# Two layers of a decoder trunk: layer 1's projections run four steps ahead through one queue, and a head's row of maxima comes by transposes alone

## The chip, the cores and the metric

The kernel runs on one core of one Trainium2 chip. The metric is the device time of one execution in microseconds (us); the time of a kernel is the median of its runs. A difference of 0.3% (9.2 us here) is about what a measurement of this kernel can tell from no change.

## What is computed

Two layers on x of 2048 rows by 1024 columns, float32. Layer 0 is a gated linear recurrence beside a pooling mixer. Layer 1, which the change touches, is attention with 16 heads of 64 columns, cut to:

```
proj = h @ w_in                                  # q, k, v, gate, forget logit
q, k = rms_norm per head;  cumf = cumsum(log_sigmoid(fl + b_f))
logits = q·k * scale + cumf[query] - cumf[key]   # causal
o = softmax(logits) @ v * silu(gate);  x = x + gate * (o @ w_out)
```

A softmax over a row may have any one number taken from all logits of the row: the quotient stays the same. The kernel takes the row's maximum, so that the exponentials stay in range.

## The kernel before

The 2048 rows go in four segments s = 0 to 3 of 512. For each segment layer 0 runs, then layer 1. The 512 new queries of a segment meet the keys of segments 0 to s; old keys and values come back from DRAM (`k1d`, `k2d`, `vd`). A product of float32 numbers is made of several fp32r products of a high and a low part, so a projection step is 24 matmuls (8 depth blocks by 3 passes) of 256 columns.

**One head of layer 1.** `prep` transposes the projected q and k of a head (`pqkT`) and builds four operands. `Q1` and `K1` hold 64 rows of the high part and 64 of the low part. `Q3` and `K2` hold the rest in 68 rows: 64 of high part, and four more. In these four, `K2` has the forget sum's high and low part and two rows of ones, `Q3` has two rows of ones and two rows for the negated maximum's high and low part. These last two rows are zero at first (a transfer from `q4d`). `max_pass` multiplies `Q3` by `K2` in blocks (`pmx`), takes the maximum of each on VectorE (`mxs`, `m`: 128 queries by 4 blocks), makes a negated high and low part (`mh`, `mhl`), turns them by one transpose into 8 rows of 128 (`pmt`), copies these to SBUF (`mr`) and sends them by a transfer from ScalarE's queue into rows 66 and 67 of `Q3`. `attend` then adds two products per block of 128 keys in PSUM (`pst`), of which the second reads `Q3` with these rows, takes exponentials twice on ScalarE (`ph` in fp32r, and `pst` in float32), their difference on VectorE (`pl`), a running sum on GpSimd (`la`), and multiplies by the values (`pov`, `pol`).

**The order.** The program is written as generators that are interleaved, and the framework orders each engine's instructions ahead of time from it. `quad_attention` runs four heads; while head h attends, the maxima of head h+1 are taken step by step, the last part of `max_pass` (from `pmt` on) comes behind `attend`, and `prep` of head h+2 behind that. `need` takes steps of the fill until a result is there. The fill of a quad of four heads is `quad_fill`: 16 steps of projections (q and k of a pair of heads, a gate, the next pair, the next quad's values), spread over the yields of the four heads by `weave`, and used up at the end of the quad. Each quad makes a new `Steps` queue. Since the 16 steps are spread over four heads, the q and k that `prep` needs behind an even head are projected during that very head. In the last quad of s = 0 to 2 the fill goes on with the first part of the next segment's layer 0 (`pre0`), in that of s = 3 with the output projection (`out_most`). The first head's maxima are taken ahead of quad 0, beside two steps of the values.

Of the kernel before, what the change touches and what calls it, by code (L numbers as in the profile page):

```python
# [8 lines left out]
F32 = mybir.dt.float32  # L9
# [9 lines left out]
P = 128  # L19
# [6 lines left out]
NH = 16  # L26
HD = 64
VW = 2 * HD + 2
EPS = 1e-6
NEG = -1e30  # L30

# [2 lines left out]
def trunk(ctx, tc, x, cvec, norm_g, ada_c, ada_w, ada_b, ada_bg, lbp, w0, w0o, w1, w1f, w1o,  # L34
# [115 lines left out]

    x1d = dr.tile([T, D], F32, name="x1d")
    k1d = dr.tile([NH, P, T], F32, name="k1d")
    k2d = dr.tile([NH, HD + 4, T], F32, name="k2d")
    vd = dr.tile([NH, P, T // P, VW], F32, name="vd")
    cfd = dr.tile([NH, 4, T], F32, name="cfd")
    q4d = dr.tile([4, SEG], F32, name="q4d")
    gd = dr.tile([2, D], F32, name="gd")


# [816 lines left out]
    def forget_rows(s, act):  # L976
        pf = ps_pj("pfl")

        for d in range(ND):
            for b in range(2):  # L980
                mm(pf[0:48, :], wf[:, d, :], act[:, d, b, :], start=(d + b == 0), stop=(d + b == ND))
        z = tmp("z")[0:NH]
        S.activation(z, pf[0:NH, :], AF.Identity, bias=fb)
        V.tensor_tensor(z, pf[32:32 + NH, :], z, op=ALU.add)
        a = tmp("za")[0:NH]
        S.activation(a, z, AF.Abs)
        S.activation(a, a, AF.Exp, scale=-1.0)
        S.activation(a, a, AF.Ln, bias=1.0)

        V.scalar_tensor_tensor(z, z, 0.0, a, op0=ALU.min, op1=ALU.subtract)  # L990
        cf = tmp("cf")[0:NH]
        V.tensor_tensor_scan(cf, z, zero1[0:NH].to_broadcast([NH, SEG]), fcar, op0=ALU.add, op1=ALU.add)
        V.tensor_copy(fcar, cf[:, SEG - 1:SEG])
        V.tensor_scalar(cf, cf, -1.0, None, op0=ALU.mult)
        ch_ = tmp("cfh", F32R)[0:NH]
        V.tensor_copy(ch_, cf)
        cl = tmp("cfl", F32R)[0:NH]
        split_lo(cl, cf, ch_)
        nc.sync.dma_start(cfd[:, 0, s * SEG:(s + 1) * SEG], f(ch_))
        nc.sync.dma_start(cfd[:, 1, s * SEG:(s + 1) * SEG], f(cl))  # L1000

    seg1 = [dict() for _ in range(NSEG)]

# [53 lines left out]
    def prep(s, h):  # L1057

        L = seg1[s]
        qk = L["qk", h // 2]  # L1060
        j = h % 2
        pt = ps_misc("pqkT")
        for tb in range(NTB):
            transpose(pt[:, tb * P:(tb + 1) * P], qk[:, tb, j * P:(j + 1) * P])
        lo, up = slice(0, HD), slice(HD, P)
        g = col["qkg"]
        Q1 = qp.tile([P, SEG], F32R, name="Q1", tag="qa")
        Q3 = qp.tile([P, SEG], F32R, name="Q3", tag="qb")
        K1 = kp.tile([P, SEG], F32R, name="K1", tag="k1c")
        K2 = kp.tile([P, SEG], F32R, name="K2", tag="k2c")  # L1070
        S.activation(Q1[lo], pt[lo], AF.Copy, scale=g[lo])
        S.activation(K1[up], pt[up], AF.Copy, scale=g[up])
        V.scalar_tensor_tensor(Q1[up], pt[lo], g[lo], f(Q1[lo]), op0=ALU.mult, op1=ALU.subtract)
        V.scalar_tensor_tensor(K1[lo], pt[up], g[up], f(K1[up]), op0=ALU.mult, op1=ALU.subtract)
        S.copy(Q3[lo], f(Q1[lo]))
        S.copy(K2[lo], f(K1[up]))
        nc.scalar.dma_start(f(Q3[HD:HD + 4]), q4d)
        nc.scalar.dma_start(f(K2[HD:HD + 4]), cfd[h, :, s * SEG:(s + 1) * SEG])
        if s < NSEG - 1:
            nc.sync.dma_start(k1d[h, :, s * SEG:(s + 1) * SEG], f(K1))  # L1080
            nc.sync.dma_start(k2d[h, :, s * SEG:(s + 1) * SEG], f(K2[0:HD + 4]))
        L["ops", h] = (Q1, Q3, K1, K2)

    def old_k2(h, c):
        K2 = kp.tile([P, SEG], F32R, name="K2o", tag="k2o", bufs=3)
        nc.sync.dma_start(f(K2[0:HD + 4]), k2d[h, :, c * SEG:(c + 1) * SEG])
        return K2

    def max_pass(s, h):

        _, Q3, _, K2 = seg1[s]["ops", h]
        mxs = small([P, NTB, NSEG], "mxs")
        for c in range(s + 1):
            kc = K2 if c == s else old_k2(h, c)
            for i in range(NTB):
                n = SEG if c < s else (i + 1) * P
                pm = ps_mx("pmx")
                mm(pm[:, 0:n], Q3[0:HD + 4, i * P:(i + 1) * P], kc[0:HD + 4, 0:n], start=True, stop=True)
                if c < s:
                    V.tensor_reduce(mxs[:, i, c:c + 1], pm[:, 0:n], axis=AX.X, op=ALU.max)  # L1100
                else:
                    V.tensor_tensor_reduce(pm[:, 0:n], pm[:, 0:n], mq[:, SEG - n:], 1.0, NEG, op0=ALU.add,
                                           op1=ALU.max, accum_out=mxs[:, i, c:c + 1])
                if c < s or i < NTB - 1:
                    yield
        m = small([P, NTB], "m")
        V.tensor_reduce(m, mxs[:, :, 0:s + 1], axis=AX.X, op=ALU.max)
        mhl = small([P, 2, NTB], "mhl")
        mh = small([P, NTB], "mh", F32R)
        V.tensor_scalar(mh, m, -1.0, None, op0=ALU.mult)  # L1110
        V.tensor_copy(mhl[:, 0, :], f(mh))
        V.scalar_tensor_tensor(mhl[:, 1, :], m, -1.0, f(mh), op0=ALU.mult, op1=ALU.subtract)
        yield
        pt = ps_misc("pmt")
        transpose(pt[0:2 * NTB, 0:P], mhl.rearrange("p a b -> p (a b)"))
        mr = sp.tile([2 * NTB, P], F32R, name="mr", tag="mr", bufs=1)
        V.tensor_copy(mr, pt[0:2 * NTB, 0:P])
        nc.scalar.dma_start(f(Q3[HD + 2:HD + 4].rearrange("a (b t) -> a b t", t=P)), f(mr))

    def attend(s, h):  # L1120

# [17 lines left out]
        for c in range(s + 1):  # L1139
# [8 lines left out]
            for b in range(NTB):  # L1148
                q0 = 0 if c < s else b * P
                ks = slice(b * P, (b + 1) * P)  # L1150
                st = ps_st("pst")
                mm(st[:, q0:], k1[:, ks], Q1[:, q0:], start=True, stop=False)
                mm(st[:, q0:], k2[0:HD + 4, ks], Q3[0:HD + 4, q0:], start=False, stop=(c < s))
                if c == s:
                    mm(st[:, q0:q0 + P], identb, mk, start=False, stop=True)
                ph = tmp("ph", F32R)
                S.activation(ph[:, q0:], st[:, q0:], AF.Exp)  # L1157
                S.activation(st[:, q0:], st[:, q0:], AF.Exp)  # L1158
                pl = tmp("pl", F32R)
                split_lo(pl[:, q0:], st[:, q0:], ph[:, q0:])  # L1160
                if kb == 0:
                    first = f(ph)
                    if s == 0:
                        G.tensor_copy(la, first)
                elif kb == 1 and s > 0:
                    G.tensor_tensor(la, first, f(ph), op=ALU.add)
                else:
                    G.tensor_tensor(la[:, q0:], la[:, q0:], f(ph[:, q0:]), op=ALU.add)  # L1168
                todo.append((b, q0, kb, vv, ph, pl))
                if len(todo) > LAG:  # L1170
                    values(*todo.pop(0))
                kb += 1
                yield
# [32 lines left out]
        L["pairs"] = pair + 1  # L1206

    LAG = 2

    def quad_attention(s, quad, fill):  # L1210

# [21 lines left out]
    def layer1(s, xs):  # L1233
# [12 lines left out]
        prep(s, 0)  # L1246
        next(vq)
        prep(s, 1)
        fill = Steps()
        fill.add(vq, 2)  # L1250
        fill.add(quad_fill(s, 0), 16)
        weave(max_pass(s, 0), NTB * (s + 1) + 1, fill, keep=16)
        L["mix"] = big.tile([P, ND, 2, SEG], F32R, name="o1", tag="act")
        for quad in range(4):
            if quad:
                fill = Steps()
            more = quad == 3 and s + 1 < NSEG
            if more:
                pre = pre0(s + 1)
                fill.add(take(pre, 2), 2)  # L1260
            n = 16 if quad < 3 else 8
            if s == 0 and quad == 1:
                fill.add(both(quad_fill(s, quad), ada_gate1()), n + 9)
            elif quad:
                fill.add(quad_fill(s, quad), n)
            if more:
                fill.add(pre, NPRE - 2)
            elif quad == 3:
                fill.add(out_most(s, L), 14)
            weave(quad_attention(s, quad, fill), 16 * (s + 1), fill, keep=2 if more else 0)  # L1270
        finish(s, NH - 1)
        fill.drain()
        if s == NSEG - 1:
# [8 lines left out]
    def constants():  # L1282
# [15 lines left out]
        V.memset(o1, 1.0)  # L1298
        z1 = tmp("z1")
        V.memset(z1, 0.0)  # L1300
        nc.sync.dma_start(q4d[0:2, :], o1[0:2])
        nc.sync.dma_start(q4d[2:4, :], z1[0:2])
        for s in range(NSEG):
            nc.sync.dma_start(cfd[:, 2, s * SEG:(s + 1) * SEG], o1[0:NH])
            nc.sync.dma_start(cfd[:, 3, s * SEG:(s + 1) * SEG], o1[0:NH])
        wfr = tmp("wfr", F32, (P, ND, NH))
        nc.sync.dma_start(wfr, w1f)
        V.tensor_copy(wf[:, :, 0:NH], wfr)
# [80 lines left out]
```

## Time and profile before

| | |
|---|---|
| median of 3 runs | 3062.76 us (3058.55 to 3068.89) |
| the profiled execution | 3059.16 us, span 3057.4 us |
| TensorE busy | 2799.8 us (92% of the span), mean granted clock 0.975 |
| VectorE, ScalarE, GpSimd busy | 2373.8, 1792.8, 1191.7 us |

The span is the time from the first to the last instruction. Each engine works off its instructions in order and waits at one whose input is not there yet; the profile names the instruction that ended the wait. Matmuls are pipelined: the busy time of one counts until its result is there, while the next has begun already.

### The profile page before, as it was taken

Reading aid. Unit: us, or ns where it says so; the run is one execution under the profiler, and the core shown is the slowest. Engines: PE = TensorE matmul, PEld = TensorE weight load, DVE = VectorE, ACT = ScalarE, POOL = GpSimd, SP = SyncE. Lnnn points to the kernel's source line nnn. Section 1 sums busy time; section 2 is a strip of 40 time slices with the busy share of each in tenths; the row PEclk is TensorE's granted clock in tenths of the full one; section 3 lists DMA queues with packets and bytes.
Section 4 is the critical chain, followed back from the end, with each engine's and each line's share of the span. In section 5 each row is a group of like instructions: output and inputs, shape, how many; then the busy total and the mean of one; then the engine's idle time right before and its main releaser. Section 6 shows DMA issues by size and latency. Waiting matters only on the chain.

```text
span 3057.4 us, 49147 instructions
## 1 busy us (share of the span) xinstructions
PE 2799.8 (92%) x17020; PEld 2378.7 (78%) x17020; DVE 2373.8 (78%) x4646; ACT 1792.8 (59%) x3679; POOL 1191.7 (39%) x992
## 2 busy tenths in 40 slices
PE   4999898999998898999999899989999999999998
PEld 4888877879887777779888677777888977676767
DVE  8877688867676888876677888888758688888886
ACT  3454566763545666674445666667544566666674
POOL 3321233323212444434111555554421246655565
PEclk9999999999999999999999999999999999999999
DMA  6423454424234334434234343443333323333342
GB/s 247 163 78 104 120 141 106 122 77 128 73 114 111 101 96 109 130 90 135 68 102 118 111 108 115 117 125 106 115 99 94 110 90 101 103 96 99 92 135 79
DMA packets 198904, 338.56 MB, mean 111 GB/s; under 512 B 19768, under 2 KB 67000, under 8 KB 196096
## 3 DMA queue, kind: packets, MB, share of 16 engines
q1 hardware_dynamic: 195264, 321.52, 36.3%
q10 hardware_dynamic: 3392, 13.90, 1.3%
q8 instruction: 135, 2.21, 0.3%
q14 instruction: 113, 0.93, 0.1%
HBM read 285.72 MB, written 49.36 MB: 110 GB/s over the span
## 4 chain that ended last, share of the span: by engine, by line
PE 49%; DVE 16%; DMA 6%; ACT 5%; issue 3%; POOL 0%; SPq 0%; DVEq 0%; ACTq 0%; POOLq 0%
PE py L40 9%; PE pst L40 6%; PE pgt L40 6%; PE pqk L40 6%; PE pv L40 4%; PE pmx L40 3%; DMA K2o<-k2d 3%; PE pov L40 3%; PE pol L40 2%; PE pq L40 2%; DVE pl L182 2%; PE pl L40 2%; PE pf L40 2%; DVE wt L182 2%; DMA Q<-mr 2%
## 5 line engine op out<-in xcount | busy, mean ns | idle before, releaser
L182 POOL TENSOR_TENSOR wt<-raw,wt 128x512 fp32r<-128x512 f32 x287 | 431.3, 1511 | 998.1 <-ACT wt L293 931.9
L1168 POOL TENSOR_TENSOR la<-la,ph 128x512 f32<-128x512 f32 (+3 forms) x528 | 614.6, 1164 | 445.4 <-ACT ph L1157 396.5
L1157 ACT ACTIVATE ph<-pst 128x512 fp32r<-128x512 f32 (+3 forms) x640 | 341.6, 534 | 277.6 <-PE pst L40 258.6
L182 DVE TENSOR_TENSOR pl<-pst,ph 128x512 fp32r<-128x512 f32 (+3 forms) x640 | 385.7, 604 | 123.2 <-ACT pst L1158 111.1
L40 PE MATMUL pqk<-wt,h 128*128 128x256 f32 x3072 | 457.4, 286 | 5.7 <-DVE h L495 2.6
L40 PEld LDWEIGHTS pqk<-wt,h 128*128 128x128 f32 x3072 | 426.4, 192 | 29.8 <-DVE h L495 3.4
L40 PE MATMUL pgt<-h,wt 128*128 128x512 f32 x1536 | 418.5, 406 | 0.2 <-ACT e L527 0.2
L293 ACT CAST wt<-raw 128x512 fp32r<-128x512 f32 x578 | 337.3, 622 | 72.2 <-PE py L40 33.3
L40 PE MATMUL pv<-wt,h 128*128 128x256 f32 x2304 | 346.9, 295 | 6.0 <-DVE h L182 4.3
L40 PEld LDWEIGHTS pv<-wt,h 128*128 128x128 f32 x2304 | 324.1, 200 | 22.7 <-DVE h L182 6.4
L1158 ACT ACTIVATE pst<-pst 128x512 f32<-128x512 f32 (+3 forms) x640 | 340.1, 531 | 0.0
L40 PEld LDWEIGHTS pgt<-h,wt 128*128 128x128 f32 x1536 | 290.4, 194 | 62.0 <-issue 1.9
L182 DVE TENSOR_TENSOR wt<-raw,wt 128x512 fp32r<-128x512 f32 x291 | 264.2, 912 | 54.7 <-ACT wt L293 53.2
L1100 DVE TENSOR_REDUCE mxs<-pmx 128x1 f32<-128x512 f32 x384 | 258.4, 685 | 46.9 <-PE pmx L40 43.4
L40 PE MATMUL py<-wt,o 128*128 128x256 f32 x1536 | 203.6, 287 | 1.3 <-ACT o L1204 1.2
L40 PE MATMUL py<-wt,mix 128*128 128x256 f32 x1536 | 198.4, 287 | 3.0 <-DVE yt L842 2.1
L40 PEld LDWEIGHTS py<-wt,o 128*128 128x128 f32 x1536 | 194.2, 193 | 7.0 <-ACT o L1204 1.5
L40 PEld LDWEIGHTS py<-wt,mix 128*128 128x128 f32 x1536 | 187.7, 191 | 10.7 <-issue 4.5
L40 PE MATMUL pst<-Q,K2o 68*128 68x512 f32 x384 | 150.2, 412 | 39.6 <-DMA Q<-mr 23.0
L40 PE MATMUL pst<-Q,K1o 128*128 128x512 f32 x384 | 161.9, 427 | 18.8 <-DVE pl L182 18.2
L40 PE MATMUL pov<-ph,Vo 128*128 128x512 f32 x384 | 164.5, 428 | 4.4 <-ACT ph L1157 2.9
L40 PE MATMUL pst<-Q,K 128*128 128x512 f32 (+7 forms) x512 | 131.8, 335 | 37.1 <-DVE pl L182 27.9
(254 smaller groups left out, 5307.4 us busy)
## 6 DMA issues: line engine op xcount, KB each, us to landing
raw<-in_w_dram SPq DMA_DIRECT2D x448, 256.0 KB
K2o<-k2d SPq DMA_DIRECT2D x192, 136.0 KB
Vo<-vd SPq DMA_DIRECT2D x96, 260.0 KB
K1o<-k1d SPq DMA_DIRECT2D x96, 256.0 KB
raw<-in_w1o_dram SPq DMA_DIRECT2D x66, 256.0 KB
raw<-in_w0o_dram SPq DMA_DIRECT2D x64, 256.0 KB
vd<-Vc SPq DMA_DIRECT2D x48, 260.0 KB
ada<-in_ada_w_dram ACTq DMA_DIRECT2D x12, 1024.0 KB
```

What stands on the lines that cost most here:

```text
L40: return nc.tensor.matmul(*a, **k)
L182: (eng or V).tensor_tensor(out_t, full, f(hi), op=ALU.subtract)
L293: S.copy(wt[:, 0, sl, :], raw)
L1100: V.tensor_reduce(mxs[:, i, c:c + 1], pm[:, 0:n], axis=AX.X, op=ALU.max)
L1157: S.activation(ph[:, q0:], st[:, q0:], AF.Exp)
L1158: S.activation(st[:, q0:], st[:, q0:], AF.Exp)
L1168: G.tensor_tensor(la[:, q0:], la[:, q0:], f(ph[:, q0:]), op=ALU.add)
```

## The change

1. `layer1` keeps one `Steps` queue for all four quads. `AHEAD` = 4 more steps of quad 0's fill are taken beside the first head's maxima (6 in place of 2), and each quad adds the next quad's steps ahead of its own heads and leaves four of them undone. So every projection of layer 1 comes four steps, that is one head, earlier against the heads. Quads 0 to 2 still take 16 steps each for s = 0 to 2, and quad 3 takes 28 in place of 32. For s = 3 quads 0 to 3 take 16, 16, 12 and 22. For s = 0 the sums for layer 1's gate move along with quad 1's fill.
2. The negated maximum becomes one row of `Q3` (row 64) in place of two, so there are 67 rows in place of 68 in `Q3`, `K2`, `k2d`; the rows of `cfd` and `q4d` are ordered anew, three in place of four.
3. In `max_pass` three VectorE instructions (`mh`, `mhl` twice), the copy `mr` and the transfer into `Q3` go. In their place four transposes of one column of `m` each write 512 numbers into partition 0 of `pmt`, and one ScalarE instruction copies these, times -1, into row 64 of `Q3`.

```diff
+KR = HD + 3
...
-    k2d = dr.tile([NH, HD + 4, T], F32, name="k2d")
+    k2d = dr.tile([NH, KR, T], F32, name="k2d")
-    cfd = dr.tile([NH, 4, T], F32, name="cfd")
-    q4d = dr.tile([4, SEG], F32, name="q4d")
+    cfd = dr.tile([NH, 3, T], F32, name="cfd")
+    q4d = dr.tile([3, SEG], F32, name="q4d")
...
     def prep(s, h):
-        nc.scalar.dma_start(f(Q3[HD:HD + 4]), q4d)
-        nc.scalar.dma_start(f(K2[HD:HD + 4]), cfd[h, :, s * SEG:(s + 1) * SEG])
+        nc.scalar.dma_start(f(Q3[HD:KR]), q4d)
+        nc.scalar.dma_start(f(K2[HD:KR]), cfd[h, :, s * SEG:(s + 1) * SEG])
...
     def max_pass(s, h):
-                mm(pm[:, 0:n], Q3[0:HD + 4, i * P:(i + 1) * P], kc[0:HD + 4, 0:n], start=True, stop=True)
+                mm(pm[:, 0:n], Q3[0:KR, i * P:(i + 1) * P], kc[0:KR, 0:n], start=True, stop=True)
...
         V.tensor_reduce(m, mxs[:, :, 0:s + 1], axis=AX.X, op=ALU.max)
-        mhl = small([P, 2, NTB], "mhl")
-        mh = small([P, NTB], "mh", F32R)
-        V.tensor_scalar(mh, m, -1.0, None, op0=ALU.mult)
-        V.tensor_copy(mhl[:, 0, :], f(mh))
-        V.scalar_tensor_tensor(mhl[:, 1, :], m, -1.0, f(mh), op0=ALU.mult, op1=ALU.subtract)
         yield
         pt = ps_misc("pmt")
-        transpose(pt[0:2 * NTB, 0:P], mhl.rearrange("p a b -> p (a b)"))
-        mr = sp.tile([2 * NTB, P], F32R, name="mr", tag="mr", bufs=1)
-        V.tensor_copy(mr, pt[0:2 * NTB, 0:P])
-        nc.scalar.dma_start(f(Q3[HD + 2:HD + 4].rearrange("a (b t) -> a b t", t=P)), f(mr))
+        for i in range(NTB):
+            transpose(pt[0:1, i * P:(i + 1) * P], m[:, i:i + 1])
+        S.activation(Q3[HD:HD + 1], pt[0:1], AF.Copy, scale=-1.0)
...
+    AHEAD = 4
...
     def layer1(s, xs):
         fill = Steps()
         fill.add(vq, 2)
         fill.add(quad_fill(s, 0), 16)
-        weave(max_pass(s, 0), NTB * (s + 1) + 1, fill, keep=16)
+        weave(max_pass(s, 0), NTB * (s + 1) + 1, fill, keep=16 - AHEAD)
         L["mix"] = big.tile([P, ND, 2, SEG], F32R, name="o1", tag="act")
+        more = s + 1 < NSEG
         for quad in range(4):
-            if quad:
-                fill = Steps()
-            more = quad == 3 and s + 1 < NSEG
-            if more:
+            before = fill.n
+            if quad == 2 and more:
                 pre = pre0(s + 1)
                 fill.add(take(pre, 2), 2)
-            n = 16 if quad < 3 else 8
-            if s == 0 and quad == 1:
-                fill.add(both(quad_fill(s, quad), ada_gate1()), n + 9)
-            elif quad:
-                fill.add(quad_fill(s, quad), n)
-            if more:
+            if s == 0 and quad == 0:
+                fill.add(both(quad_fill(s, 1), ada_gate1()), 16 + 9)
+            elif quad < 3:
+                fill.add(quad_fill(s, quad + 1), 16 if quad < 2 else 8)
+            elif more:
                 fill.add(pre, NPRE - 2)
-            elif quad == 3:
+            else:
                 fill.add(out_most(s, L), 14)
-            weave(quad_attention(s, quad, fill), 16 * (s + 1), fill, keep=2 if more else 0)
+            ahead = AHEAD if more or quad < 2 else 0
+            keep = fill.n - before - ahead if quad < 3 else 2 if more else 0
+            weave(quad_attention(s, quad, fill), 16 * (s + 1), fill, keep=keep)
```

## Rows read from the trace of the kernel before

**Rows 1.** The page: busy us, share of the span, instructions of each engine.

```profile
span 3057.4 us, 49147 instructions
PE 2799.8 (92%) x17020; PEld 2378.7 (78%) x17020; DVE 2373.8 (78%) x4646; ACT 1792.8 (59%) x3679; POOL 1191.7 (39%) x992
```

**Rows 2.** The waits of TensorE: us in total, times, longest.

```profile
PE pst L40 <- DVE pl L182: 46.1, 61, 3.4
PE pqkT L43 <- DVE qk L1022: 31.2, 27, 2.9
PE pst L40 <- DMA Q<-mr: 30.9, 14, 6.3
PE pmt L43 <- DVE mhl L1112: 19.0, 20, 1.7
```

**Rows 3.** The timeline of TensorE where layer 1 starts (s = 0 to 2).

```profile
368.19 0.79 PE L40 MATMUL pst<-Q,K 68*128 68x512 f32 x1 [4.78 <-DMA Q<-mr]
...
976.19 1.22 PE L40 MATMUL pst<-Q,K2o 68*128 68x512 f32 x2 [5.42 <-DMA Q<-mr]
...
1685.08 1.22 PE L40 MATMUL pst<-Q,K2o 68*128 68x512 f32 x2 [6.34 <-DMA Q<-mr]
```

**Rows 4.** The chain that ended last: start, us, what.

```profile
1086.56 2.88 PE pqk L40 x24
...
1675.83 9.21 DMA Q<-mr
```

**Rows 5.** Stretches of 5 us at s = 1: busy of each engine, granted clock, DMA.

```profile
960.00:965.00 5.00, 5.00 (x41) 4.87 (x41) 3.93 (x12) 2.83 (x6) 1.89 (x2) 1.00 0.43 136
...
970.00:975.00 5.00, 0.77 (x7) 0.57 (x5) 0.94 (x3) 0.00 (x0) 0.00 (x0) 0.80 0.98 163
975.00:980.00 5.00, 3.81 (x15) 3.52 (x16) 2.17 (x6) 2.09 (x4) 1.29 (x1) 0.52 0.41 117
```

**Rows 6.** VectorE's timeline behind a head of s = 3.

```profile
2564.91 0.16 DVE L1107 TENSOR_REDUCE m<-mxs 128x4 f32<-128x16 f32 x1
...
2567.00 0.77 DVE L1110 TENSOR_SCALAR mh<-m 128x4 fp32r<-128x4 f32 x1
...
2568.28 0.95 DVE L1111 COPY mhl<-mh 128x4 f32<-128x4 f32 x1
2569.15 0.15 DVE L1112 SCALAR_TENSOR_TENSOR mhl<-m,mh 128x4 f32<-128x4 f32 x1
```

**Rows 7.** TensorE's timeline at that head and a later one.

```profile
2569.36 0.27 PE L43 MATMUL pmt<-ident,mhl 128*8 128x128 f32 x1 [1.53 <-DVE mhl L1112]
...
2857.40 0.37 PE L43 MATMUL pmt<-ident,mhl 128*8 128x128 f32 x1 [1.54 <-DVE mhl L1112]
```

**Rows 8.** Stretches of 2.5 us there, columns as in rows 5.

```profile
2570.00:2572.50 2.50, 2.50 (x13) 2.36 (x13) 1.19 (x3) 0.94 (x2) 0.48 (x2) 0.58 0.65 248
2572.50:2575.00 2.50, 2.50 (x15) 2.40 (x15) 2.37 (x5) 1.19 (x3) 0.00 (x0) 0.73 0.00 0
...
2857.50:2860.00 2.50, 2.50 (x12) 2.40 (x12) 0.65 (x3) 0.58 (x1) 1.02 (x2) 0.50 0.82 266
```

**Rows 9.** TensorE's timeline: transposes of q and k, at three of the 64 heads.

```profile
341.81 1.11 PE L43 MATMUL pqkT<-ident,qk 128*128 128x128 f32 x4 [2.72 <-DVE qk L1022]
...
953.17 0.60 PE L43 MATMUL pqkT<-ident,qk 128*128 128x128 f32 x4
...
2447.36 0.98 PE L43 MATMUL pqkT<-ident,qk 128*128 128x128 f32 x4 [1.85 <-DVE qk L1022]
```

**Rows 10.** Groups by line: busy us, mean ns, idle before.

```profile
L1199 ACT ACTIVATE u<-pL 128x512 f32<-128x512 f32 x32 | 19.1, 597 | 17.8 <-PE pL L40 16.9
...
L43 PE MATMUL pmt<-ident,mhl 128*8 128x128 f32 x64 | 17.7, 277 | 19.2 <-DVE mhl L1112 19.0
```

**Rows 11.** The waits of ScalarE.

```profile
ACT ph L1157 <- PE pst L40: 258.6, 253, 8.8
...
ACT Q L1071 <- PE pqkT L43: 53.5, 31, 4.7
```

More of the change, by code (lines that the diff above doesn't have):

```diff
@@ L998, in forget_rows @@
         split_lo(cl, cf, ch_)
-        nc.sync.dma_start(cfd[:, 0, s * SEG:(s + 1) * SEG], f(ch_))
-        nc.sync.dma_start(cfd[:, 1, s * SEG:(s + 1) * SEG], f(cl))
+        nc.sync.dma_start(cfd[:, 1, s * SEG:(s + 1) * SEG], f(ch_))
+        nc.sync.dma_start(cfd[:, 2, s * SEG:(s + 1) * SEG], f(cl))
     seg1 = [dict() for _ in range(NSEG)]
@@ L1076, in prep @@
         S.copy(K2[lo], f(K1[up]))
-        nc.scalar.dma_start(f(Q3[HD:HD + 4]), q4d)
-        nc.scalar.dma_start(f(K2[HD:HD + 4]), cfd[h, :, s * SEG:(s + 1) * SEG])
+        nc.scalar.dma_start(f(Q3[HD:KR]), q4d)
+        nc.scalar.dma_start(f(K2[HD:KR]), cfd[h, :, s * SEG:(s + 1) * SEG])
         if s < NSEG - 1:
             nc.sync.dma_start(k1d[h, :, s * SEG:(s + 1) * SEG], f(K1))
-            nc.sync.dma_start(k2d[h, :, s * SEG:(s + 1) * SEG], f(K2[0:HD + 4]))
+            nc.sync.dma_start(k2d[h, :, s * SEG:(s + 1) * SEG], f(K2[0:KR]))
         L["ops", h] = (Q1, Q3, K1, K2)
@@ L1085, in old_k2 @@
         K2 = kp.tile([P, SEG], F32R, name="K2o", tag="k2o", bufs=3)
-        nc.sync.dma_start(f(K2[0:HD + 4]), k2d[h, :, c * SEG:(c + 1) * SEG])
+        nc.sync.dma_start(f(K2[0:KR]), k2d[h, :, c * SEG:(c + 1) * SEG])
         return K2
@@ L1152, in attend @@
                 mm(st[:, q0:], k1[:, ks], Q1[:, q0:], start=True, stop=False)
-                mm(st[:, q0:], k2[0:HD + 4, ks], Q3[0:HD + 4, q0:], start=False, stop=(c < s))
+                mm(st[:, q0:], k2[0:KR, ks], Q3[0:KR, q0:], start=False, stop=(c < s))
                 if c == s:
@@ L1300, in constants @@
         V.memset(z1, 0.0)
-        nc.sync.dma_start(q4d[0:2, :], o1[0:2])
-        nc.sync.dma_start(q4d[2:4, :], z1[0:2])
+        nc.sync.dma_start(q4d[1:3, :], o1[0:2])
+        nc.sync.dma_start(q4d[0:1, :], z1[0:1])
         for s in range(NSEG):
-            nc.sync.dma_start(cfd[:, 2, s * SEG:(s + 1) * SEG], o1[0:NH])
-            nc.sync.dma_start(cfd[:, 3, s * SEG:(s + 1) * SEG], o1[0:NH])
+            nc.sync.dma_start(cfd[:, 0, s * SEG:(s + 1) * SEG], o1[0:NH])
         wfr = tmp("wfr", F32, (P, ND, NH))
```

## The prediction, made before the changed kernel had run

> **What bounds the kernel now.** I read the page first, then TensorE's waits, then the chain of waits that ended last, then the timeline and the stretches around the longest waits. The page shows TensorE busy for 2799.8 of 3057.4 us, so 257.6 us are left in which it does nothing; the next engine is VectorE with 78% [rows 1]. The reader is to see a kernel in which no other engine is near the end of its time, but in which TensorE is held up for short moments. A change can gain there: by a smaller idle time of TensorE, by less work for it, and by the clock that it is granted.
>
> TensorE's waits name who holds it up [rows 2]. Three of the first four are ends of chains that this change shortens: 31.2 us on the scaled q and k (`pqkT`), 30.9 us on the transfer that brings the maxima into `Q3`, 19.0 us on the pair `mhl`. The first one, 46.1 us on `pl`, is VectorE's pace, and the change speaks to it only in passing.
>
> The timeline where layer 1 starts shows the largest single waits of all: 4.78, 5.42 and 6.34 us for s = 0, 1 and 2, 16.5 of the 30.9 us [rows 3]. The chain has the transfer itself as its longest piece there, with 9.21 us from issue to landing at s = 2 [rows 4]: 4 KB that come late; at s = 1 the transfer engines are 98% busy meanwhile [rows 5]. Nothing is left for TensorE to do meanwhile. [...]
>
> **What is removed, and its cost.**
>
> *The transfer of the maxima.* It gives way to one instruction of ScalarE that reads what the transposes left. The trace of before has no such instruction of 1 by 512; the nearest row is a ScalarE pass over 128 by 512 out of PSUM, 0.60 us [rows 10]. I take 0.6 us, as if one partition cost what 128 do; with four transposes (0.6 us for four, [rows 9]) the row is there some 1.3 us after `m`, against 9 us at the worst. The wait of 30.9 us [rows 2] can't give more than itself; I take 29, and for the range 15 (the three starts hardly count less) to 30.9. The lost clock behind it: three starts at 1.8 us [rows 5], and as an estimate 2.6 us for the eleven other waits, which have 14.4 us together; that makes 8 us, 4 to 10 for the range.
>
> *The pair `mhl`.* In s = 3 `m` is there at 2564.91, but `mh` starts at 2567.00, the copy at 2568.28, the low part at 2569.15: three tiny instructions, of which two take 0.77 and 0.95 us, and each with larger work of VectorE ahead of it [rows 6]. The transpose starts at 2569.36 after TensorE had waited 1.53 us [rows 7]. After the change the transposes need `m` alone, 4.2 us earlier. Of the 19.0 us [rows 2] I take 15, since some `m` will still come late; 8 to 19 for the range. Behind this wait too the clock falls: 0.58 and 0.73 in the two stretches of 2.5 us, which is 1.7 us of work [rows 8]; it does so at five heads of s = 3, the first and the last of which are shown [rows 7, 8]. That gives 8 us, 4 to 9 for the range.
>
> *The scaled q and k.* A pair's projections end now at the end of the head behind which they are needed; then VectorE still has the norm to work out, and TensorE stands at `pqkT`: 31.2 us in 27 waits [rows 2]. Four of these are at the starts of layer 1 (2.72 us in s = 0 is the first, 1.85 us in s = 3 the last, 8.4 us in all four [rows 9]); there `prep` follows its projection at once, and the change moves nothing. The other 22.8 us go if the projection is one head earlier. What is late next is VectorE, whose work on q and k stays and now lies beside the head's own; I take 17 us, 8 to 22.8 for the range.
>
> **What is added.** Four transposes take the place of one, 192 more in all. Four transposes of q and k in a row take 0.60 us, one alone has 0.27 us until its result is there [rows 9, 10], so each further one adds (0.60 − 0.27) / 3 = 0.11 us. That makes 192 × 0.11 = 21 us, all on TensorE, which is the bound; I count it whole. The lower bound is the same sum with a third of it in moments when TensorE would have waited anyway, 14 us; the upper one is that they don't overlap at all, 192 × 0.277 = 53 us [rows 10].
>
> [...]
>
> ScalarE gets 64 × 0.6 = 38 us more. I cost it at nothing: the work that hides it is TensorE's, for which ScalarE waits 258.6 us before the exponentials [rows 11], and the first exponential of a head needs the row anyway. If that cover is gone it costs up to the full 38 us. Without the transfer ScalarE's queue issues 64 transfers fewer, and behind it nothing else waits. VectorE loses four small instructions per head, 2 us at the head shown [rows 6]; that would shorten the 46.1 us on `pl` [rows 2], and I count nothing, with 10 us of gain as the other end. The row in 67 in place of 68 partitions changes no number of columns: nothing either way.
>
> **What is moved.** Four steps of 2.88 us each [rows 4], 11.5 us per segment, go from quad 3 (quad 2 in s = 3) to the first head's maxima; with them go their weight loads on SP's queue, the copies and differences of these weights on ScalarE, GpSimd and VectorE, one head earlier too, and for s = 0 to 2 two loads of x, in quad 2. TensorE has the same work in sum. At s = 1 it is busy for 5.00 of 5 us in the stretch ahead of the first maxima [rows 5], so four more steps lengthen that stretch; but what they push back is the place where TensorE waits 5.42 us today, and they are then missing from quads in which it waits least. I take nothing for it; 46 us (4 × 11.5) is the bound of a loss, if the quads get no shorter.
>
> **The sum.** 29 + 8 + 15 + 8 + 17 = 77 us gained, 21 us spent: 56 us. 3059.2 − 56 = 3003 us for an execution like the profiled one. The median of the runs lies 0.12% above it (3062.76 to 3059.16), so I forecast 3006 us.
>
> **The rivals.**
>
> *The transposes don't overlap.* For it: they are small, and each loads other weights; the row of a transpose alone is 0.277 us [rows 10]. Against it: four of q and k overlap, with larger weights [rows 9]. 32 us less gain: 3038 us.
>
> *The moved steps lengthen the starts.* For it: TensorE is full ahead of the first maxima [rows 5], and the heads behind may go at the pace of VectorE (46.1 us of waits on `pl` [rows 2]), so that missing steps don't shorten them. Against it: TensorE is the busiest engine by 14 points [rows 1]. 46 us less gain: 3052 us.
>
> *The waits go over to VectorE.* The 17 and 15 us and their clock come back as waits on `pl`, and only the transfer's terms are left. For it: `pl` is the longest wait already, and VectorE's small instructions take up to 0.95 us. Against it: VectorE loses work by this change. 29 + 8 − 21 = 16 us of gain, less a quarter of the 46 us of the moved steps: 4 us of gain, 3058 us on the scale of the median, no change that can be measured.
>
> *ScalarE is held up by the row.* This one ends slower. ScalarE works in order; if its new copy stands ahead of a head's last exponentials and waits there for transposes that lie behind a fill step on TensorE, the exponentials wait too, then the values' products, then TensorE. The nearest price: ScalarE waits 53.5 us in 31 times for the transposes of q and k, 1.7 us each [rows 11]. 64 × 1.7 = 109 us, of which I let two thirds reach TensorE: 73 us, and 3006 + 73 = 3079 us. It decides from (56 + 9) / 64 = 1.0 us per head on. Against it: the transfer stood at the same place of the same queue, waited for the same transpose, and no such wait of ScalarE is among its longest.
>
> **How the numbers follow.** A difference of 0.3%, 9 us, is what a measurement tells from none, so faster is below 3053.6 and slower above 3071.9. I give the forecast 62 in 100, transposes that don't overlap 8, longer starts 12, waits that go over to VectorE 8, ScalarE held up 10. Faster are the first two and 8 of the 12 of longer starts: 78 in 100. Within 0.3% lie 3 of these and 6 of VectorE's 8: 9 in 100. Slower are ScalarE's case and 3 in which two losses meet: 13 in 100. The lower end: with every term at its better bound the gain is 30.9 + 10 + 19 + 9 + 22.8 + 10 − 14 = 88 us, which is 2975 us on the scale of the median; fill that is ready earlier may cover a quarter of the 46.1 us on `pl` too, and so I take 2964. The upper end takes in the longer starts (3052) and VectorE's case (3058), so 3060; ScalarE's case, a little below the lower end and what else there is stay out, under 2 in 10. The forecast's own range is 2964 to 3030.
>
> **What would show it.** In the changed kernel's TensorE waits the one on a transfer into `Q` is gone, the one on `mhl` becomes a smaller one on `m`, and `pqkT` keeps some 8 us of its four starts. The stretch behind the start of s = 1 has no clock of 0.52 and no 5 us of idle TensorE. `pmt` shows 256 transposes 0.11 us apart. I am wrong if ScalarE's waits name `pmt` with over 60 us, if the wait on `pl` grows by over 30 us, or if the starts are longer by more than the quads are shorter.

## The result: 9.1% slower

The changed kernel takes 3343.2 us (median of 4 runs, 3335.7 to 3347.2) beside 3064.7 us for the kernel before in the same session. The ratio is 1.0908, interval 1.0880 to 1.0935. The forecast was 3006 us, and the range ended at 3060: it is wrong by 337 us, and no rival came near. The profiled execution has a span of 3334.0 us, and a granted clock of 0.933 where it was 0.975.

The page of the changed kernel, as in [rows 1]:

```profile
span 3334.0 us, 49234 instructions
...
PE 2903.1 (87%) x17212; PEld 2456.9 (74%) x17212; DVE 2299.4 (69%) x4390; ACT 1828.7 (55%) x3743; POOL 1171.8 (35%) x992
```

TensorE is busy for 103 us more and idle for 431 us in place of 258. Who holds it up stands in its waits (us in total, times, longest), as in [rows 2]:

```profile
PE pst L41 <- DMA K2o<-k2d: 197.0, 47, 8.9
PE pst L41 <- DVE pl L183: 42.1, 25, 11.0
PE pst L41 <- ACT Q L1113: 21.1, 10, 11.2
...
PE pqkT L44 <- DVE qk L1023: 9.2, 6, 2.6
```

Of the three waits that the change was to shorten, that on `mhl` is 1.5 us on `m` now, and that on `pqkT` fell from 31.2 to 9.2 us. The wait on the transfer of the maxima (30.9 us) is gone, but 21.1 us on the new row stand in its place. And a wait that the prediction does not speak of stands above all others: 197.0 us on the load of old keys, `K2o`. Before, it was the fifth:

```profile
PE pst L40 <- DMA K2o<-k2d: 16.4, 19, 2.0
```

The chain of work that ended last in the changed kernel gives the length of single loads (start, us, what):

```profile
1902.01 11.15 DMA K2o<-k2d
...
3030.69 8.51 DMA K2o<-k2d
3061.52 7.64 DMA K2o<-k2d
```

The timeline of SP and of TensorE, and the two stretches of 5 us from 2666 us on, around one such load of s = 3 (columns as in [rows 5]):

```profile
2663.57 0.32 SPq L1087 DMA_DIRECT2D K2o<-k2d  x1
```

```profile
2669.03 0.50 PE L41 MATMUL pst<-Q,K2o 67*128 67x512 f32 x1 [3.80 <-DMA K2o<-k2d]
```

```profile
2666.00:2671.00 5.00, 1.97 (x7) 1.60 (x8) 0.38 (x2) 1.09 (x2) 1.88 (x2) 0.89 0.24 79
2671.00:2676.00 5.00, 2.99 (x10) 1.99 (x9) 2.96 (x5) 2.17 (x4) 3.13 (x3) 0.77 0.40 122
```

The reader is to see a load of 134 KB that is under way for over 5 us while the transfer engines are busy for a quarter of their time (the last but one column, 0.24). So it is not the total traffic that makes it late, as it was at the start of s = 1 before, with 98% [rows 5]. And the granted clock falls behind the wait, to 0.77 in the second stretch. What a lower clock costs shows at the same place: a product of 512 columns takes 0.40 us ahead of the wait, at 2664.84 us, where the granted clock is 1.00, and 0.63 us behind it, at 2670.87, where it is 0.50.

Where the time is lost in the run shows from the timelines of TensorE, cut at the first product of a segment's layer 1 (`pfl`) and at its first and last turned maximum (`pmt`), in us, summed over the four segments. "Start" is from `pfl` to the first `pmt`, "heads" from there to the last `pmt`, "rest" to the next `pfl`, or to the end of TensorE's work. What lies ahead of the first `pfl` is left out. The kernels named e... are those of the next section. These are single profiles, and the runs of one kernel in one session lie 4 to 33 us apart, so differences of a few us here show nothing.

| kernel | starts | heads | rest |
|---|---|---|---|
| before | 116.1 | 1683.7 | 921.0 |
| changed | 136.5 | 1947.4 | 916.9 |
| e1, 68 rows | 137.5 | 1654.1 | 908.3 |
| e7, queue alone | 145.8 | 1677.1 | 914.6 |
| e6, transposes alone | 112.9 | 1675.1 | 916.7 |
| e10, transposes, 64 and 3 rows | 116.0 | 1649.6 | 916.3 |
| e4, all, 64 and 3 rows | 136.3 | 1616.3 | 910.1 |
| e11, as e4, four steps later | 113.7 | 1642.8 | 909.8 |
| e12, as e4, stores of 67 rows | 138.8 | 1679.1 | 910.9 |

The loss lies in the heads, and there in s = 2 and 3, where most old keys are loaded: 465.8 and 538.3 us before, 575.4 and 673.6 after.

### The profile page after: what moved, and what is told of

Its sections match the earlier page's. It is cut to its first block, busy times and chain, and to the rows that moved or that the text cites. A ratio compares the mean times of both kernels' runs of the same rounds, so it can differ in the third digit from the quotient of the medians.

```text
span 3334.0 us, 49234 instructions
## 1 busy us (share of the span) xinstructions
PE 2903.1 (87%) x17212; PEld 2456.9 (74%) x17212; DVE 2299.4 (69%) x4390; ACT 1828.7 (55%) x3743; POOL 1171.8 (35%) x992
## 4 chain that ended last, share of the span: by engine, by line
PE 56%; DMA 18%; DVE 12%; ACT 9%; issue 3%; SPq 1%; POOL 1%; ACTq 0%; DVEq 0%; POOLq 0%
DMA K2o<-k2d 14%; PE py L41 9%; PE pgt L41 9%; PE pst L41 6%; PE pqk L41 6%; PE pv L41 5%; PE pmx L41 4%; PE pov L41 3%; PE pol L41 3%; PE pf L41 2%; PE pl L41 2%; PE pq L41 2%; ACT wt L294 1%; PE pL L41 1%; DMA raw<-in_w_dram 1%
## 5 line engine op out<-in xcount | busy, mean ns | idle before, releaser
L1163 POOL TENSOR_TENSOR la<-la,ph 128x512 f32<-128x512 f32 (+3 forms) x528 | 603.4, 1143 | 693.8 <-ACT ph L1152 648.8
L41 PE MATMUL pqk<-wt,h 128*128 128x256 f32 x3072 | 447.6, 291 | 5.3 <-DVE h L496 2.6
L41 PE MATMUL pgt<-h,wt 128*128 128x512 f32 x1536 | 408.1, 407 | 0.1
L41 PE MATMUL pst<-Q,K2o 67*128 67x512 f32 x384 | 181.1, 473 | 208.5 <-DMA K2o<-k2d 197.0
L41 PEld LDWEIGHTS pst<-Q,K2o 67*128 67x128 f32 x384 | 83.9, 219 | 238.3 <-DMA K2o<-k2d 212.1
L41 PE MATMUL pmx<-K2o,Q 67*128 67x512 f32 x384 | 175.8, 463 | 33.4 <-DMA K2o<-k2d 11.5
L41 PE MATMUL pst<-Q,K1o 128*128 128x512 f32 x384 | 173.0, 452 | 26.3 <-DVE pl L183 26.0
```

What stands on the lines that cost most here:

```text
L41: return nc.tensor.matmul(*a, **k)
```

## The experiments

The theory: the step "the row in 67 in place of 68 partitions changes no number of columns" looked at TensorE alone. The same row also goes from 68 to 67 in the loads and stores of `k2d`, and a transfer of 67 rows is slow. The rival: the row count is innocent, and it is the new order of the transfers (steps ahead, one transfer fewer) that makes old keys late.

**e1: the changed kernel with 68 rows.** A 68th row is all zeros in `Q3` and all ones in `K2`, so it adds nothing.

```diff
-KR = HD + 3
+KR = HD + 4
...
-    cfd = dr.tile([NH, 3, T], F32, name="cfd")
-    q4d = dr.tile([3, SEG], F32, name="q4d")
+    cfd = dr.tile([NH, 4, T], F32, name="cfd")
+    q4d = dr.tile([4, SEG], F32, name="q4d")
```

> The changed kernel with a 68th row put back into Q3 (zeros) and K2 (ones), so that the transfers of K2 have 68 rows as before; queue and transposes stay changed. Theory A (a transfer of 67 rows lands several us later than one of 68, and that alone costs the 279 us): 3064 us or less, about 3006 us if the forecast's other terms hold, and the waits of TensorE on K2o fall from 197 us to some 16 us. Theory B (the steps moved ahead put weight loads in front of the loads of K2 on SP's queue; the number of rows is innocent): within 1% of 3343 us, waits on K2o still near 200 us.

Measured: 3036.0 us, ratio to before 0.9905 (0.9877 to 0.9933). One more row, which adds nothing, takes 0.1003 × 3064 = 307 us off the changed kernel; the waits on `K2o` fall to 22.2 us, so the rival falls. Its page and TensorE's waits:

```profile
span 3033.9 us, 49233 instructions
...
PE 2815.5 (93%) x17212; PEld 2389.7 (79%) x17212; DVE 2299.9 (76%) x4390; ACT 1826.5 (60%) x3743; POOL 1183.9 (39%) x992
```

```profile
PE pst L41 <- DVE pl L183: 33.3, 30, 2.4
PE pst L41 <- DMA K2o<-k2d: 22.2, 21, 3.9
...
PE pqkT L44 <- DVE qk L1023: 10.1, 6, 2.7
PE pst L41 <- ACT Q L1113: 7.5, 9, 2.9
```

Of the 300 us between the two spans, 175 are waits of `pst` on old keys (197.0 − 22.2), 88 are the longer busy time of as many matmuls (2903.1 − 2815.5) at a mean granted clock of 0.933 in place of 0.976, 14 the waits on the new row. The other 23 us are spread over smaller waits.

**e2 and e3: the kernel before, with its load and store of 68 rows cut in two,** 67 and 1 in e2, 64 and 4 in e3; the computation is the same.

```diff
-            nc.sync.dma_start(k2d[h, :, s * SEG:(s + 1) * SEG], f(K2[0:HD + 4]))
+            nc.sync.dma_start(k2d[h, 0:HD, s * SEG:(s + 1) * SEG], f(K2[0:HD]))
+            nc.sync.dma_start(k2d[h, HD:HD + 4, s * SEG:(s + 1) * SEG], f(K2[HD:HD + 4]))
...
-        nc.sync.dma_start(f(K2[0:HD + 4]), k2d[h, :, c * SEG:(c + 1) * SEG])
+        nc.sync.dma_start(f(K2[0:HD]), k2d[h, 0:HD, c * SEG:(c + 1) * SEG])
+        nc.sync.dma_start(f(K2[HD:HD + 4]), k2d[h, HD:HD + 4, c * SEG:(c + 1) * SEG])
```

> The kernel before, with each load and store of K2 from and to DRAM cut in two, 67 rows and 1 row; nothing else. Theory A: slower than 3200 us, with some 200 us of waits of TensorE on K2o. Theory B: 3064 us, at most 20 us more for 240 more transfers on SP's queue.

> The kernel before, with each load and store of K2 cut in two, 64 rows and 4 rows; as many transfers as with 67 and 1. Theory A: 3064 us or a little less, since 64 rows spread better than 68 (the 16 us of waits on K2o may go: 3045 to 3064 us). Theory B: the same as 67 and 1.

Measured: e2 3478.7 us, ratio 1.1348 (1.1295 to 1.1401); e3 3024.4 us, ratio 0.9889 (0.9824 to 0.9953). Both have the same number of transfers and bytes, so it is not their number. TensorE's waits in e2:

```profile
PE pst L40 <- DMA Q<-mr: 145.5, 46, 12.4
PE pst L40 <- DMA K2o<-k2d: 126.5, 39, 7.5
```

The waits that end with the transfer of the maxima are 145.5 us there in place of 30.9 [rows 2]. Not all of that is this transfer: the longest, 12.4 us, ended 4.8 us after the transfer had been issued, so most of it was a wait for something ahead of it. But the transfer, which has 4 KB of its own and is issued from ScalarE's queue, has become slower. A head of s = 3 in e2, its issue and the product that reads the row, and then the same before:

```profile
2726.70 0.62 ACTq L1120 DMA_DIRECT2D Q<-mr  x1
2731.61 0.77 PE L40 MATMUL pst<-Q,K2o 68*128 68x512 f32 x1 [1.99 <-DMA Q<-mr]
```

```profile
2605.38 0.65 ACTq L1118 DMA_DIRECT2D Q<-mr  x1
2608.44 0.63 PE L40 MATMUL pst<-Q,K2o 68*128 68x512 f32 x2
```

In 14 of the 16 heads of s = 3 TensorE goes on 4.5 to 5.1 us after the issue in e2, each time after a wait for this transfer; before, it read the row 2.6 to 4.4 us after the issue and did not wait. So the slow transfers hold up one of another shape and queue. This falls on the rival too: the kernel of before, with its own order, loses even more (416 us) from 67 rows and 1 than the changed one from 67 (307 us); why it loses more was not tried. e3 is 21 us below the range that I had named for it.

**e4: the changed kernel with loads and stores cut into 64 and 3 rows,** the edit of e3 in the changed kernel.

> The changed kernel with each load and store of K2 cut in two, 64 rows and 3 rows. Theory A: as the kernel with 68 rows or up to 15 us faster, near 3000 us. Theory B: within 1% of 3343 us or slower, for there are 240 more transfers on the queue that it blames.

Measured: 3009.5 us, ratio 0.9813 (0.9765 to 0.9861). The waits on `K2o` are 7.5 us in 5 times. It has 192 loads and 48 stores more than e1, and is 27 us faster, where I had expected at most 15: 68 rows are slow too. e4 also has a tensor `k2d` of 67 rows in DRAM and is quick, and e2 has one of 68 and is slow; so it is the transfer's rows, and not where the data lie in DRAM.

**e5 and e9: loads by themselves.** Both kernels compute nothing of the reference; they load n rows of 2 KB eight times for each n and let VectorE read one column of each. e5 also loads 128 rows right behind 64, 67, 68 and 80. The loop of e9:

```python
    for n in (64, 66, 67, 68, 72, 80, 96, 128):
        for rep in range(8):
            t = sp.tile([P, D], F32, name=f"r{n}", tag="r")
            nc.sync.dma_start(t[0:n, 0:C], x[rep * P:rep * P + n, 0:C])
            V.tensor_copy(seen[0:n, rep:rep + 1], t[0:n, 0:1])
```

> The disputed transfer by itself: nothing of the reference is computed; loads of n rows of 2 KB from DRAM into SBUF one at a time, n = 64, 66, 67, 68, 72, 80, 96, 128, eight of each, each waited for by a copy on VectorE; then loads of 64, 67, 68 and 80 rows with a load of 128 rows right behind on the same queue, and the copy waits for the latter. The times are from issue to the copy. [...] Theory A2 (an uneven number of rows or one that is no multiple of four is slow): 66 rows are as slow as 67. Theory C (the time goes by bytes): 128 rows are the slowest, 67 lies 5% above 64. [...]

In e5 loads from three series went on beside each other, so that its waits for the other row counts can't be laid to one load; 67 rows were waited for 48.8 us in eight times, 68 rows 22.6 us. How long 128 rows behind the others take can't be read from it either. e9 has one buffer, so one load is under way at a time.

> This kernel computes nothing of the reference: it loads 64, 66, 67, 68, 72, 80, 96 and 128 rows of 512 float32 numbers eight times each, one load at a time, each waited for by VectorE. Theory, that the number of rows decides over how many transfer engines a load is spread (67 and 66 badly, 68 fairly, 64, 72, 80, 96 and 128 well): the load of 67 rows is waited for some 3 us longer than that of 64, 68 lies between, and 128 rows come sooner than 67. Rival, that a transfer's time goes by its bytes or that 67 rows suffer only among other transfers: 67 rows lie between 66 and 68 within 0.2 us, and 128 are the slowest. [...]

The groups by line and shape in e9; the idle time before the copies is eight times the wait for a load:

```profile
L26 DVE COPY seen<-r 128x1 f32<-128x1 f32 x8 | 1.2, 154 | 22.7 <-DMA r<-in_x_dram 22.7
L26 DVE COPY seen<-r 68x1 f32<-68x1 f32 x8 | 1.2, 150 | 27.9 <-DMA r<-in_x_dram 27.9
L26 DVE COPY seen<-r 66x1 f32<-66x1 f32 x8 | 1.2, 150 | 18.7 <-DMA r<-in_x_dram 18.7
L26 DVE COPY seen<-r 67x1 f32<-67x1 f32 x8 | 1.2, 150 | 60.4 <-DMA r<-in_x_dram 60.4
...
L26 DVE COPY seen<-r 64x1 f32<-64x1 f32 x8 | 1.2, 146 | 21.1 <-DMA r<-in_x_dram 21.1
```

That is 7.55 us for 67 rows, 3.49 for 68, 2.34 for 66, 2.64 for 64 and 2.84 for 128, with nothing else under way; 72, 80 and 96 rows take 2.48, 2.39 and 2.53. A load of 67 rows takes 2.7 times as long as one of 128, so the rival, time by bytes, falls. My theory had 66 rows among the slow ones, and that fell too. The stretches of the loads of 64, 66, 67 and 68 rows, in this order (the last columns are the granted clock, the mean busy share of 16 transfer engines, and GB/s):

```profile
1.00:23.20 22.20, 1.13 (x8) 0.00 (x0) 1.00 0.16 47
23.20:43.10 19.90, 1.23 (x9) 0.00 (x0) 1.00 0.17 54
43.10:104.70 61.60, 1.20 (x9) 0.00 (x0) 1.00 0.05 18
104.70:133.70 29.00, 1.20 (x8) 0.00 (x0) 1.00 0.12 38
```

One engine that is always busy would give a share of 1/16 = 0.06; the loads of 67 rows give 0.05. Over one load that is 0.05 × 16 × 7.7 us = 6.2 us of engine work, for 66 rows 0.17 × 16 × 2.5 = 6.8 us: about the same work. By these shares 0.8 of the 16 engines are busy on the mean for 67 rows, 1.9 for 68, 2.7 for 66 and 2.6 for 64, so as an estimate the work of the slow loads is shared out less. No view here shows the number of engines itself, and why 67 and 68 rows take longer was not shown.

Among 66, 72 and 64 rows the number makes no difference for a load of this size (2.34, 2.48 and 2.64 us). That 68 rows are slow and 66 are not speaks against a rule by odd and even; no other odd number was tried by itself.

**e8: one transfer of 80 rows,** of which 13 are zeros that are written to `k2d` once at the start; the stores are cut into 64 and 3.

```diff
+MR = HD + 16
...
-    k2d = dr.tile([NH, KR, T], F32, name="k2d")
+    k2d = dr.tile([NH, MR, T], F32, name="k2d")
...
-        nc.sync.dma_start(f(K2[0:KR]), k2d[h, :, c * SEG:(c + 1) * SEG])
+        nc.sync.dma_start(f(K2[0:MR]), k2d[h, :, c * SEG:(c + 1) * SEG])
...
+            if s < NSEG - 1:
+                for r in range(KR, MR):
+                    nc.sync.dma_start(k2d[:, r, s * SEG:(s + 1) * SEG], z1[0:NH])
```

> The changed kernel with one load of 80 rows in place of 67 (13 rows of zeros more, which no product reads; stores cut in 64 and 3 rows). Theory A: at least as fast as with loads of 64 and 3 rows, 3009 us or less, with 19% more bytes per load than 67 rows. Theory C (bytes): slower than with 67 rows.

Measured: 3022.1 us, ratio 0.9854 (0.9833 to 0.9875). That is 13 us more than I had expected, and still 321 us faster than 67 rows, with a fifth more rows and bytes. The wait on `K2o` is not among TensorE's ten longest. The 39 transfers of zeros cost at the start: layer 1 of s = 0 begins at 352.2 us, in e4 at 332.1.

**e12: loads cut into 64 and 3, stores left whole with 67 rows.**

> The changed kernel with the 192 loads of old keys cut into 64 and 3 rows, and the 48 stores left whole with 67 rows. Theory, that the loss is TensorE's waiting for loads, and that a store, for which nothing waits soon, may take its 7.5 us: 3009 us as with both cut, within 10 us, and the waits of TensorE on old keys stay below 15 us. Rival, that a transfer of 67 rows holds up others, whoever waits for it: 48 of the 240 slow transfers are left, so a fifth of the loss of some 334 us, 67 us, comes back: 3076 us.

Measured: 3063.8 us, ratio 0.9998 (0.9983 to 1.0014). My theory, that only loads are waited for, fell, and the waits on `K2o` are 32.7 us in place of at most 15: the 48 stores alone cost 54 us beside e4, 1.1 us each, and the 192 whole loads, by which alone the changed kernel differs from e12, another 279 us, 1.5 us each. The rival had 67 us for the stores. The heads of s = 3, which store nothing, take 502.6 us, as in e4 (502.5); those of s = 2 take 496.4 in place of 454.3. The timeline of SP and TensorE, a piece of the chain, and the stretches behind such a store:

```profile
1789.83 0.24 SPq L1082 DMA_DIRECT2D k2d<-K  x1
...
1793.75 1.70 SPq L1088 DMA_DIRECT2D K2o<-k2d  x1
```

```profile
1793.75 9.93 DMA K2o<-k2d
```

```profile
1803.82 0.77 PE L41 MATMUL pst<-Q,K2o 67*128 67x512 f32 x1 [6.60 <-DMA K2o<-k2d]
```

```profile
1798.00:1803.00 5.00, 0.00 (x0) 0.00 (x0) 0.38 (x1) 0.00 (x0) 0.00 (x0) 0.59 0.55 119
1803.00:1808.00 5.00, 4.18 (x15) 3.83 (x16) 2.10 (x5) 2.09 (x4) 2.56 (x2) 0.50 0.22 69
```

The store is issued at 1789.83 (L1082). The load of three rows behind it (L1088) takes 9.93 us from issue to landing, and between 1798 and 1803 nothing runs but 0.38 us of VectorE. Between the two, a load of 64 rows and two stores of `vd` go out on the same queue. They do so in e4 as well, in the same order; there the same load of three rows takes 5 us, and at the two other places like it 5.4 and 5.6 us (8.4 and 10.5 in e12):

```profile
1754.72 4.99 DMA K2o<-k2d
```

So it is the store of 67 rows that adds some 3 to 5 us to a load of three rows. By what way the one holds up the other, no view here shows.

**e6 and e7: the two parts of the change, each alone, with 68 rows.** e6 is e1 with the queue of before, e7 the kernel before with the queue of after.

> The transposes and the single row alone, with 68 rows in the transfers, and the queue of the kernel before. By the forecast's terms (29 + 8 for the transfer of the maxima, 15 + 8 for the pair, 21 spent): 39 us faster than before, 3023 us. If the transposes are what gave less than was forecast: 3050 us or more. If the queue is: 3036 us or less, that is no slower than both parts together with 68 rows.

> The queue with four steps ahead alone, on the kernel before with its transfer of the maxima and 68 rows. By the forecast's term: 17 us faster than before, 3045 us, and the wait on pqkT falls from 31 to some 8 us. If the moved steps lengthen the starts: slower than before by up to 29 us.

Measured: e6 3040.4 us, ratio 0.9923 (0.9909 to 0.9937); e7 3077.4 us, ratio 1.0040 (1.0024 to 1.0056). By the terms of the forecast e6 was to be 39 us faster than before and is 24; e7 was to be 17 us faster and is 12 slower, as I had named it for the case that the moved steps lengthen the starts. TensorE's waits in e6, then in e7:

```profile
PE pst L41 <- DVE pl L183: 41.1, 43, 2.9
PE pst L41 <- DMA K2o<-k2d: 29.6, 22, 5.9
PE pqkT L44 <- DVE qk L1023: 26.0, 23, 2.7
```

```profile
PE pst L40 <- DMA Q<-mr: 33.5, 14, 6.7
PE pst L40 <- DVE pl L182: 26.9, 47, 1.5
...
PE pqkT L43 <- DVE qk L1022: 10.4, 5, 3.6
```

The queue alone cuts `pqkT` to 10.4 us and `pl` to 26.9, and is still 12 us slower: its starts are 30 us longer, its heads only 7 us shorter. Why a start gets longer even than the work moved there shows on VectorE at s = 2 of e7:

```profile
1694.78 0.17 DVE L1107 TENSOR_REDUCE m<-mxs 128x4 f32<-128x12 f32 x1
1698.05 0.69 DVE L182 TENSOR_TENSOR wt<-raw,wt 128x512 fp32r<-128x512 f32 x1 [3.10 <-ACT wt L293]
```

`m` is ready at 1694.95, but the weights of a projection step stand ahead of `mh` on VectorE and are not there yet: 3.10 us, and TensorE waits 4.17 us for `mhl`. In e1 the same thing sits on ScalarE at s = 2: the new row stands behind a weight copy that waits 2.57 us for its load, and TensorE waits 2.92 us.

**e10 and e11: the parts again, with loads of 64 and 3 rows.** e10 is e4 with the queue of before; e11 is e4 without the four steps beside the first head's maxima, so that quad 0 takes 20 steps and the lead is there from quad 1 on.

```diff
-        weave(max_pass(s, 0), NTB * (s + 1) + 1, fill, keep=16 - AHEAD)
+        weave(max_pass(s, 0), NTB * (s + 1) + 1, fill, keep=16)
```

> The row by transposes with loads and stores cut into 64 and 3 rows, and the queue of before. Theory, that the moved steps lengthen the starts by some 22 us and give back no more than that in the heads: 3000 to 3012 us, no slower than the same with the queue four steps ahead (3009). Rival, that with quick loads of old keys the steps ahead pay: 3014 us or more (3040 of the transposes alone with 68 rows, less the 26 us that 64 and 3 rows gave beside the queue).

> The changed kernel with loads and stores cut into 64 and 3 rows, and with none of the four extra steps beside the first head's maxima: the first quad takes 20 steps in place of 16 and the lead is there from the second quad on. Theory, that the four steps cost what they lengthen the start by, since the heads run at other engines' pace: the starts fall back by some 20 us in sum, the heads of the first quads take up to 46 us more work into their own waits, 2990 to 3005 us. Rival, that TensorE's work is what sets the pace everywhere and the place of the steps is all the same: 3009 us, within 8 us.

Measured: e10 3020.0 us, ratio 0.9856 (0.9833 to 0.9878); e11 3009.1 us, ratio 0.9827 (0.9807 to 0.9846). Both of my theories fell here. e10 is 11 us above e4 and e11, so with quick loads the queue seems to pay; but the interval of e10 overlaps with those of both. And e11 is as fast as e4: the starts of e4 are 23 us longer than those of e11 and its heads 27 us shorter. Where the four steps lie makes no difference that can be measured.

## Why the prediction was wrong

**The step that failed.** "The row in 67 in place of 68 partitions changes no number of columns: nothing either way." It costs 307 us (e1 against the changed kernel). The count of columns is right for TensorE: at a granted clock of 1.00 a product of 512 columns takes 0.40 us with 67 rows (changed kernel, at 2661.58 us) and 0.39 with 68 (before, at 2600.02). But the row count is also that of 192 loads and 48 stores, and a transfer of 67 rows takes 7.55 us alone where one of 68 takes 3.49 (e9). In the heads of s = 3, where nothing is stored, 21 of the 29 loads of old keys on the chain take 7.2 to 8.6 us, about that length, the longest 11.6; before, the longest took 5.7. In s = 2, where stores of 67 rows go beside them, 10 of 15 take 11 to 12.2 us. The prediction costed the transfers that the change removes and moves, and not those whose shape it changes; and as no row of the trace before has a transfer of 67 rows, the step should have had bounds from both sides.

**The rest of the sum.** Without that step e1 shows the rest: 29 us gained (20 to 38 by its interval) where 56 were forecast. The three waits did fall by about what was forecast, but TensorE's idle time fell by two thirds of that only, by 39 us (257.6 to 218.4) where 29 + 15 + 17 = 61 were forecast: other waits grew.

- *The transfer of the maxima.* 30.9 us of wait are gone; 7.5 us at `pst` and 2.1 us at `pqkT` come back on the new row in e1, so 21 where I took 29. The row takes 0.586 us, forecast 0.6, as this view of the tile in the changed kernel shows (ns least, median, longest):

```profile
L1113 ACT ACTIVATE Q<-pmt x64: 585/586/588, 359.4 to 3285.0; 1x512 fp32r<-1x512 f32 x64
```

- *The pair `mhl`.* 19.0 us fell to 1.5 us on `m` in e1: 17.5, where I took 15. (Of the three small instructions in [rows 6] the last has no larger work of VectorE ahead of it, as the prediction has it, but only the copy.)
- *The scaled q and k.* 31.2 us fell to 10.1 in e1 and 10.4 in e7: 21, where I took 17. But much of the wait goes over to the next link. `prep` makes `Q3` and `K2` from what `pqkT` holds, and `pmx` reads them. TensorE's waits of `pmx` on these operands and the transfers into them are 6.2 us before and 13.3 in e7, 10.5 in e6 and 21.7 in e1, 6.8 in e10 and 20.2 in e4; the second of each pair has the new queue. The longest of these, before and in e1:

```profile
PE pmx L40 <- ACT K L1076: 3.3, 8, 0.6
```

```profile
PE pmx L41 <- ACT Q L1076: 10.4, 20, 1.5
```

  So 7 to 13 us of what the queue takes off `pqkT` (16 to 21 us) come back one step further on, and not on `pl`. The prediction said that VectorE would be late next; it took too little for this, and the longest of these waits in e1 is on ScalarE.
- *The transposes.* Four in a row take 0.60 us, as forecast; they overlap, and the rival that they don't did not come. The first head's at s = 1, on TensorE's timeline in the changed kernel:

```profile
986.92 0.60 PE L44 MATMUL pmt<-ident,m 128*1 128x128 f32 x4
```

- *The clock.* TensorE's busy time in e1 is 15.7 us above that of before, where 21 − 8 − 8 = 5 were forecast. If the transposes cost their 21 us, 5 of the 16 us of clock came; the mean granted clock is 0.976 beside 0.975. Clock and work can't be parted further in this difference. The 1.8 us at each start are an estimate, the 3.81 us of busy time in the stretch at a clock of 0.52 [rows 5], times the missing 0.48; no run shows them by themselves.
- *The moved steps* were costed at nothing, and that was too little. The starts of e1 are 21 us longer, the heads 30 us and the rest 13 us shorter; with 3 us ahead of the first `pfl` that sums up to the 24 us between the spans. e7 shows the queue alone to lose 12 us: its starts are longer by more than its heads are shorter, which the prediction had named as a sign of being wrong. On top of the transposes the queue gives 4 us with 68 rows (e6 to e1, within their intervals) and some 11 with 64 and 3, where the starts are 20 us longer too, but the heads 33 us shorter (e10 to e4). So what the queue wins in the heads it gives back in the starts, and whether anything is left depends on how quick the transfers are.
- *VectorE's pace.* `pl` fell from 46.1 to 33.3 us in e1; that rival did not come.
- *ScalarE held up by the row.* It did not come: ScalarE waits 10.0 us for the transposes in the changed kernel (10.4 in e1), where over 60 were named as the sign. The reverse came, the row held up by ScalarE's queue. In the changed kernel the first row of s = 2 stands behind a weight copy that waits 10.84 us for its load, and TensorE waits 11.21 us for the row: over half of the 21.1 us.

**The starts,** as in [rows 3], at s = 2 of the changed kernel, on ScalarE and on SP's queue, and then on TensorE:

```profile
1711.74 1.89 ACT L294 CAST wt<-raw 128x512 fp32r<-128x512 f32 x3 [10.84 <-DMA raw<-in_w_dram]
1713.65 0.58 ACT L1113 ACTIVATE Q<-pmt 1x512 fp32r<-1x512 f32 x1
```

```profile
1693.11 11.02 SPq L1048 DMA_DIRECT2D vd<-Vc  x3
1704.17 3.85 SPq L289 DMA_DIRECT2D raw<-in_w_dram  x4
```

```profile
1714.29 0.80 PE L41 MATMUL pst<-Q,K2o 67*128 67x512 f32 x1 [11.21 <-ACT Q L1113]
```

The load is late since SP needed 11.02 us to issue the three stores ahead of it; behind those stand the weights, behind the weights the row. The wait of 6.34 us that the change was to remove has given way to one of 11.21. The start of s = 1 is alike: a load of weights takes 10.23 us on the chain, TensorE waits 11.05 us (on `pl`), and the granted clock falls to 0.50, where the prediction had said that neither the wait nor the low clock would be left. In e1 no wait of `pst` in the whole run is longer than 3.9 us.

**What is best.** The change with transfers of 64 and 3 rows (e4 3009.5, e11 3009.1 us) is 1.7 to 1.9% faster than before. By the medians most of that is not the change: e3, which only cuts the transfers of before, takes 3024.4 us, 38 of the 53 us that e4 gains in the same session. How much exactly stays open, since e3's interval is wide (one of its four runs took 3044.6 us).

Left open: what of the 27 us that e1 takes longer than e4 is the length of a load and what its hold on other transfers was not tried apart; nor was it tried whether ScalarE's queue would serve the loads better.

## What to carry to other kernels

A tile's row count counts twice: for TensorE one row less is nothing (0.40 us a product with 67 rows, 0.39 with 68), but a transfer's time hangs on it, and not in the order of the bytes (7.55 us for 67 rows, 3.49 for 68, 2.84 for 128). When an edit changes a shape, look for every transfer of that shape and cost it by rows, not by bytes; a tail of a few rows goes into a transfer of its own, or is padded (ratios 0.9813 in e4 and 0.9854 in e8, where 67 rows gave 1.0908). And where a transfer is late while the transfer engines are a quarter busy (0.24 here), look at that transfer's shape before you blame traffic. And when a link of a chain comes earlier, ask what then waits at the next link: here 7 to 13 of 16 to 21 us came back there.

## What the runs showed of the hardware

- Eight loads of 64, 66, 67, 68 and 128 rows of 2 KB, one at a time, were waited for 2.64, 2.34, 7.55, 3.49 and 2.84 us each (e9).
- A slow transfer holds up transfers of other shapes and queues: in s = 3 the 4 KB from ScalarE's queue are there 4.5 to 5.1 us after their issue in 14 of 16 heads of e2, where 2.6 to 4.4 us were enough before, and a load of three rows behind a store of 67 took 9.93 us in e12, where it took 4.99 in e4.
- It also holds up the engine that issues. A store of `vd` has 260 KB and its shape is untouched; issuing one took SP at most 0.83 us in e4, 1.78 before, 5.25 in the changed kernel and 5.30 in e12, and everything behind it on SP's queue came later.
